# A fused block on one core: TensorE's first phase issued in traced order, with timed tasks between wide projection steps

## The chip, the core and the metric

The kernel runs on one core of a Trainium2 chip, in fp32. The metric is the device time of one execution in microseconds, lower is better. The kernel before takes 3127.56 us (median of 3 runs, 3127.19 to 3137.98).

## What is computed

One decoder block on x (2048 tokens by 1024 channels). The input is RMS-normed and modulated, then multiplied by one large input matrix. Its output feeds a convolution branch and a recurrent branch (RWKV-7), which are projected, gated, merged, projected once more and added to the residual.

```python
h = _rmsnorm(x, norm_g) * (1.0 + scale) + shift
p = h @ w_in                      # 1024 -> 73 tiles of 128 columns
c_val, c_gate, c_og, ts, r_og, g_conv, g_rwkv = split(p)
# convolution branch: causal depthwise width 31, channel LayerNorm, swish
u = layernorm(conv31(c_val * sigmoid(c_gate)) + b)
y_conv = (silu(u) * silu(c_og)) @ w_conv_out
# recurrent branch, 16 heads of 64; token shift, then per token
state = state * w_t - (state @ kk_t) b_t + v_t k_t ;  o_t = state @ r_t
y_rwkv = ((groupnorm(o) + bonus) * silu(r_og)) @ w_rwkv_out
m = sigmoid(g_conv) * y_conv + sigmoid(g_rwkv) * y_rwkv
x = x + gate * (m @ w_out);  return _rmsnorm(x, final_g)
```

## The kernel before

**Tiling.** Tokens go in four blocks of 512 (`TB`). A tile of the input projection is 128 output channels by 512 tokens, eight k-steps of 128 input channels. Every fp32 operand is split into a high and a low half; a k-step (`mm3k`, L188) multiplies high by high, high by low and low by high, and `msplit` cuts the 512 columns in two, so it issues six matmuls of 256 columns. Weight tiles come through six buffers (`load_w`, L165): in block 0 the raw tile is loaded and split by ACT (L178) and GpSimd or DVE (L180), and both halves go back to DRAM; later blocks load the halves (L171, L172). All loads are issued by SP, in order.

**First phase.** For each block there are four groups of four heads. A group has two *pairs* (`pair`, L446): decay products (L455 to L461), cumulative decays (L466), three projections K, R, V with token shift (`shifted`, L413), key norms (L493), the 64x64 decay-and-key products (L523, masked by DVE at L526 and scaled at L532), transposes (L539, L555) and a head sum (`headsum`, L272). Then the *group* (L560) inverts 32x32 triangles: DMAs take the diagonal pieces out (L581, L586), GpSimd solves them (L595, L597), DMAs bring them back (L601, L608), DVE transposes them (L624), and TensorE fills in the off-diagonal quarters (L636, L640). Then comes the *recurrence*, eight chunks of 64 tokens: TensorE L690, DVE L692, TensorE L697, DVE L710, TensorE L714, DVE L717, which writes the state that the next chunk's L690 reads. A group norm (L734 to L743) and transposes (L748) close the group. Around it lie the convolutions (`conv`, L768: two projections and 31 DVE taps, L783), the gates (`gates`, L787: four kinds of one projection each), and `xnorm` (L323), which norms and transposes the next block's input. In the last block, work of the second phase for block 0 takes the place of `xnorm` (`z_first`, `lnorm_first`).

**Second phase.** Per block: output projections of both branches (`rproj`, `cproj`, with 512 columns per matmul, `MS2`), LayerNorm (`lnorm`), the last projection (L1071 to L1073) and the final norm. Block 0's `rproj` and `cproj` run while the last recurrence ends.

**Order.** The code traces a group's pair steps in the order `ORD`, with gates and convolutions before or behind them (`FIRST`, `NEXT`, and `LP` for the last block, which keeps part of the gates for after the last group). The order in which each engine's queue is filled comes from a planner, which runs the traced program in a time model. `high_priority(HP)` lets an instruction pass others in it; `issue_after` pins a few matmuls behind one another. Queues run in the planned order.

Of the kernel before, what the change touches and what calls it, by code (L numbers as in the profile page):

```python
# [18 lines left out]
P = 128  # L19
# [12 lines left out]
KRB, TKB, ASB = 4, 3, 4  # L32
HP = 3000
WDVE, WSH = 6, 0
# [5 lines left out]
VVT, SHT, RKT, RHT, YT = "r", "sh", "k", "sh", "y"  # L40
ORD = (0, 0, 1, 0, 1, 1)
# [3 lines left out]
MS, MS2 = 2, 1  # L45
WB = 6
KEPT = ("in",)
def lplan(t):
    n = {"c": 0, "g": 0}
    r = []  # L50
    for part in t.split():
        l = []
        for w in part:
            if w != "-":
                l.append(("1234" if w == "g" else w, n[w]))
                n[w] += 1
        r.append(l)
    return r


G4 = "1234"
FIRST = (("1", 0), ("2", 0), ("3", 0), ("4", 0), ("c", 0), ("c", 1), (G4, 1))
NEXT = (("c", 0), ("1342", 0), ("c", 1), ("1342", 1))
FILL0 = (0, 1, 0, 0, 0, 0)
LP = "cgcg cgcg cc ccgg gg"
# [17 lines left out]
def hybrid_block(ctx: ExitStack, tc: tile.TileContext, x, vecs, convk, w2a2, final_g, ada, w_in, w_co, w_ro, w_o, crow, out,  # L83
# [55 lines left out]
    msplit = [MS]  # L139

# [24 lines left out]
    def load_w(name, n, hl=None):  # L165
# [10 lines left out]
        wcount[0] -= 1  # L176
        with tc.high_priority(HP):
            nc.scalar.copy(hi, st)  # L178
            lo_eng = nc.vector if wcount[0] >= 0 or (wcount[0] < -1000 and wcount[0] % 4 < W2) else nc.gpsimd
            lo_eng.tensor_tensor(out=lo, in0=st, in1=hi.bitcast(F32), op=ALU.subtract)  # L180
# [17 lines left out]
    def mm3(ps, w, a):  # L198
        for k in range(KT):
            mm3k(ps, w, a, k)  # L200

# [32 lines left out]


# [36 lines left out]
    def headsum(ps, full, hi):  # L272
        lo = e1.tile([P, TB], F32R, name="s_lo", tag="s_lo")
        nc.gpsimd.tensor_tensor(out=lo, in0=full, in1=hi.bitcast(F32), op=ALU.subtract)
        nc.tensor.matmul(ps, bones, hi, start=True, stop=False)
        nc.tensor.matmul(ps, bones, lo, start=False, stop=True)
# [46 lines left out]
    def xnorm(b, tts=range(NTT)):  # L323
        for tt in tts:
# [12 lines left out]
            for kh in range(2):  # L337
                nc.vector.tensor_scalar(out=xh[kh], in0=xh[kh], scalar1=rs, scalar2=None, op0=ALU.mult)
                pt = pl.tile([P, 4, P], F32, name="late", tag="late")
# [73 lines left out]
    def shifted(h, ti, dst):  # L413
        mi = ti - T_R
        ps = front.pop(ti, None)
        if ps is None:
            w = load_w("in", ti)
            ps = pm.tile([P, TB], F32, name="ps_main", tag="main")
            mm3(ps, w, h)
# [7 lines left out]
        nc.vector.tensor_copy(carry[:, mi:mi + 1], ps[:, TB - 1:TB])  # L427
# [18 lines left out]
    def pair(b, q_, pr, h, lora, uv, Asb, rn, res):  # L446
# [4 lines left out]
        for i in range(2):  # L451
            sl = slice(64 * i, 64 * i + 64)
            nc.gpsimd.tensor_tensor(out=wlo[sl, i, :], in0=wf[sl, i, :], in1=wl[sl, i, :].bitcast(F32), op=ALU.subtract)
        pw = pa.tile([P, TB], F32, name="aux", tag="aux")
# [20 lines left out]
        yield  # L475
# [3 lines left out]
        k = e1.tile([P, TB], F32, name="k", tag="k")  # L479
        shifted(h, T_K + pr, k)  # L480
# [3 lines left out]
        E24 = E2.rearrange("p (c e t) -> p c e t", e=2, t=CH)  # L484
        for e in range(2):
            nc.vector.scalar_tensor_tensor(out=KR[:, :, CH * (1 + e):CH * (2 + e)], in0=k4[:, :, e, :],
                                           scalar=vc("rwkv_k_k", pr), in1=E1x[:, :, e, :], op0=ALU.mult, op1=ALU.mult)
        sq = e1.tile([P, TB], F32, name="sq", tag="sq")
        nc.scalar.activation(sq, k, AF.Square, scale=vc("rwkv_k_k", pr))

# [17 lines left out]
        r = e1.tile([P, TB], F32, name="r", tag="r")  # L508
        shifted(h, T_R + pr, r)
# [4 lines left out]
        yield  # L514

        for c4 in range(NCH // 4):
            pA = [pa.tile([P, 2, 256], F32, name="aux", tag="aux") for _ in range(2)]
# [7 lines left out]
            for hh in range(2):  # L525
                nc.vector.tensor_tensor(  # L526
                    out=Asb[:, hh, c4 * 4:c4 * 4 + 4, :].rearrange("p (a e) n -> p a (e n)", e=2),
                    in0=pA[hh], in1=flat(maskA).unsqueeze(1).broadcast_to([P, 2, 256]), op=ALU.mult)
        for e in range(2):
# [3 lines left out]
                [64, 2, NCH // 2, CH]), op=ALU.mult)  # L533

        vv = e1.tile([P, TB], F32, name="vv", tag=VVT)
        shifted(h, T_V + pr, vv)
# [5 lines left out]
        pb = pa.tile([P, TB], F32, name="aux", tag="aux")  # L542
        rh = e1.tile([P, TB], F32R, name="rh", tag=RHT)
        nc.scalar.copy(rh, rk)
        headsum(pb, rk, rh)
        nc.scalar.copy(rk, pb)  # L546
# [3 lines left out]
        tk = l3.tile([P, NCH, P], F32, name="tk", tag="tk", bufs=TKB)  # L550
        for c4 in range(NCH // 4):
            pt = pa.tile([P, 4, P], F32, name="aux", tag="aux")
            for c in range(4):
                cc, e = (c4 * 4 + c) // 2, c % 2
                nc.tensor.transpose(pt[:, c, :], BK[:, cc, e * 128:e * 128 + 128], ident)  # L555
            nc.scalar.copy(tk[:, c4 * 4:c4 * 4 + 4, :], pt)
        res.update(KR=KR, tk=tk, pe=pe)
        yield

    def group(b, g, h, lora, fill):  # L560
        uv = l3.tile([P, NCH, 2, P], F32, name="uv", tag="uv", bufs=2)
        for e in range(2):
            nc.gpsimd.memset(uv[prow(e), e::2], 0.0)
        As = [l3.tile([P, 2, NCH, P], F32, name="As", tag="As", bufs=ASB) for _ in range(2)]
        R = [{}, {}]
        rn = lt.tile([P, 2, NCH // 2, 2], F32, name="rn", tag="rn")
        pairs = [pair(b, q, 2 * g + q, h, lora, uv, As[q], rn, R[q]) for q in range(2)]
        for i, q in enumerate(ORD):
            next(pairs[q])
            fill(i)  # L570


# [45 lines left out]

        pq = [p_.tile([P, 2, 2, NCH // 2, 32], F32, name=n_, tag=n_) for p_, n_ in ((pl, "late"), (pa, "aux"))]
        for e in (1, 0):  # L620
            lo_, hi_ = quarters(e)
            for q in range(2):
                for hh in range(2):
                    nc.vector.transpose(T11[lo_, q, hh], As[q][lo_, hh, e::2, lo_])  # L624
        def turns(mul):

            mm = []
            for n, (q, hh, c) in enumerate(every[::-1]):
                for e in range(2):
                    with tc.issue_after(mm[-1].ins) if mm else nullcontext():  # L630
                        mm_ = mul(e, q, hh, c, dict(start=(n == 0), stop=(n == 15), skip_group_check=True))
                    mm = mm if n else mm + [mm_]

        def lower(e, q, hh, c, kw):
            lo_, hi_ = quarters(e)
            return nc.tensor.matmul(pq[e][hi_, q, hh, c, :], As[q][lo_, hh, 2 * c + e, hi_], T11[lo_, q, hh, c, :], **kw)  # L636

        def upper(e, q, hh, c, kw):
            lo_, hi_ = quarters(e)
            return nc.tensor.matmul(pq[e][lo_, q, hh, c, :], Qs[hi_, q, hh, c, :], As[q][hi_, hh, 2 * c + e, hi_], **kw)  # L640

        turns(lower)
        for e in (1, 0):
            lo_, hi_ = quarters(e)
            nc.vector.tensor_copy(Qs[hi_], pq[e][hi_])

        turns(upper)
        for e in range(2):
            lo_, hi_ = quarters(e)
            for q in range(2):  # L650
                nc.vector.tensor_copy(As[q][lo_, :, e::2, hi_], pq[e][lo_, q])

# [3 lines left out]

# [24 lines left out]
        xcopy(0)  # L681
        for c in range(NCH):
# [4 lines left out]
            for q in range(2):  # L687
                nc.scalar.mul(Se[:, q, :], Sg[:, q, :], R[q]["pe"][:, c:c + 1])  # L688
            for q in range(2):
                nc.tensor.matmul(b_[:, q, :], R[q]["KR"][:, cc, es], Sg[:, q, :], start=(q == 0), stop=False,  # L690
                                 skip_group_check=True)
            nc.vector.tensor_tensor(out=Xz[pr_, e], in0=b_[pr_, 0:2], in1=Xz[pr_, e], op=ALU.add)  # L692


            for n, (q, hh, hs) in enumerate(every):
                with tc.issue_after(mm.ins) if n else nullcontext():
                    mm_ = nc.tensor.matmul(b_[pr_, q, hs], As[q][:, hh, c, kcol(e)], Xz[:, e, q, hs],  # L697
                                           start=(n == 0), stop=(n == 3), skip_group_check=True)
                mm = mm if n else mm_
                if c + 1 < NCH:  # L700
                    with tc.issue_after(mm.ins):
                        xval(c + 1, n)
            if c:
                with tc.issue_after(mm.ins):
                    olast(c - 1)
            if c + 1 < NCH:
                xcopy(c + 1)
            if c:
                ocopy(c - 1)
            nc.vector.tensor_tensor(out=uv[pr_, c].rearrange("p q (h n) -> p q h n", n=64),  # L710
                                    in0=b_[pr_, 0:2].rearrange("p q (h n) -> p q h n", n=64),
                                    in1=rn[pr_, :, cc, :].unsqueeze(3).broadcast_to([64, 2, 2, 64]), op=ALU.mult)
# [3 lines left out]
            for q, hh, hs in every:  # L716
# [434 lines left out]
```

## Time and profile before

| what | value |
|---|---|
| median of the runs | 3127.56 us |
| profiled execution: span, first to last instruction | 3118.7 us |
| profiled execution: its own total time | not listed apart; the runs' median is 8.9 us above the span |
| mean granted TensorE clock | 0.959 |
| busy shares | TensorE 93%, its weight loads 87%, DVE 69%, GpSimd 38%, ACT 32% |
| first phase, by the last input projection | to 2496 us |
| DMA | 667.81 MB, mean 214 GB/s |

The profile shows one execution. A row of the windows gives a stretch (from:to, in us), its length, each engine's busy time with its number of instructions, the granted clock (1.00 is full), the DMA engines' busy share and GB/s. A row of the groups gives line, engine, operation, output and inputs, shapes and count, then busy us, mean ns of one, and the idle time before them with what ended it. A row of the timeline starts with start and duration in us. A row of the waits names who waited for whom: us in total, times, longest. Overlapping matmuls make a busy TensorE look fuller than its rate is.

### The profile page before, as it was taken

The page shows a single profiled execution, that of the slowest core. Times are in us where ns is not written, and L with a number is a line of the kernel's source. Part 1 is how long each engine was busy: PE and PEld are TensorE (multiplying, and loading weights), DVE is VectorE, ACT ScalarE, POOL GpSimd, SP SyncE. Part 2 cuts the span into 40 slices and gives each one's busy share as a digit, 9 for nine tenths or more (in the row PEclk, how much of TensorE's full clock was granted, in tenths as well). Part 3 has the DMA queues.
Part 4 walks back from the last instruction along what each step waited for, and adds up shares of the span by engine and source line. Part 5 has one row for each costly group of instructions (what it writes and reads, how often), then busy time and mean ns, then how long its engine had stood idle before and what let it go on. Part 6 is the DMA issues. An engine that isn't in the chain of part 4 may idle for free.

```text
span 3118.7 us, 65148 instructions
## 1 busy us (share of the span) xinstructions
PE 2902.9 (93%) x25648; PEld 2724.8 (87%) x25648; DVE 2152.8 (69%) x4282; ACT 998.4 (32%) x1932; POOL 1170.4 (38%) x1739
## 2 busy tenths in 40 slices
PE   6789898999999989999999999999979998699998
PEld 6689898899999989899999899999979977578888
DVE  6678775686867767767677677768698446777433
ACT  4324333333333233323332424232333123343211
POOL 3265554343343425232424334416346015634000
PEclk9899999899999989999999999999989999899999
DMA  7666757474756566547565767647437668767664
GB/s 299 215 234 218 262 198 265 153 255 143 237 169 218 167 225 213 190 149 230 154 231 183 243 197 248 221 146 232 151 121 248 220 228 301 275 246 265 213 223 176
DMA packets 354852, 667.81 MB, mean 214 GB/s; under 512 B 134705, under 2 KB 153457, under 8 KB 354545
## 3 DMA queue, kind: packets, MB, share of 16 engines
q1 hardware_dynamic: 354544, 663.64, 63.3%
q8 instruction: 202, 3.31, 0.4%
q14 instruction: 106, 0.86, 0.1%
HBM read 483.07 MB, written 179.31 MB: 212 GB/s over the span
## 4 chain that ended last, share of the span: by engine, by line
PE 52%; DVE 15%; DMA 15%; POOL 8%; issue 4%; SPq 3%; ACT 3%; POOLq 0%; DVEq 0%; ACTq 0%
PE ps_main L195 37%; DMA w_st<-w_in_t 3%; PE aux L523 3%; POOL TT L597 3%; POOL itmp L595 3%; DVE acc L783 2%; DVE M L466 2%; SPq L608 2%; DMA La<-dA 1%; PE xo L697 1%; DMA dT<-TT 1%; PE pout L1072 1%; PE pout L1073 1%; PE xo L714 1%; PE pout L1071 1%
## 5 line engine op out<-in xcount | busy, mean ns | idle before, releaser
L195 PE MATMUL ps_main<-h_hi,w_hi 128*128 128x256 f32 x4608 | 961.0, 287 | 31.6 <-ACT w_hi L178 20.9
L195 PE MATMUL ps_main<-h_hi,w_lo 128*128 128x256 f32 x4608 | 964.0, 287 | 12.8 <-POOL w_lo L180 8.4
L195 PE MATMUL ps_main<-h_lo,w_hi 128*128 128x256 f32 x4608 | 965.0, 287 | 0.0
L195 PEld LDWEIGHTS ps_main<-h_hi,w_hi 128*128 128x128 f32 x4608 | 724.3, 192 | 42.3 <-ACT w_hi L178 22.2
L195 PEld LDWEIGHTS ps_main<-h_hi,w_lo 128*128 128x128 f32 x4608 | 724.3, 191 | 25.1 <-POOL w_lo L180 10.7
L195 PEld LDWEIGHTS ps_main<-h_lo,w_hi 128*128 128x128 f32 x4608 | 725.1, 192 | 8.2 <-issue 0.5
L783 DVE SCALAR_TENSOR_TENSOR acc<-u,ck,acc 128x512 f32<-128x512 f32 x928 | 698.1, 752 | 21.8
L595 POOL TENSOR_TENSOR itmp<-La,TT 128x126 f32<-128x126 f32 (+22 forms) x496 | 179.3, 361 | 162.7 <-DMA La<-dA 126.4
L717 DVE SCALAR_TENSOR_TENSOR S<-xo,pe,Se 64x64 f32<-64x64 f32 x512 | 144.5, 282 | 99.6 <-PE xo L714 90.4
L178 ACT CAST w_hi<-w_st 128x1024 fp32r<-128x1024 f32 x103 | 108.0, 1049 | 323.7 <-DMA w_st<-w_in_t 167.0
L597 POOL TENSOR_TENSOR TT<-TT,itmp 128x126 f32<-128x126 f32 (+22 forms) x496 | 188.8, 381 | 37.3
L180 POOL TENSOR_TENSOR w_lo<-w_st,w_hi 128x1024 fp32r<-128x1024 f32 x47 | 113.0, 2404 | 113.6 <-ACT w_hi L178 100.5
L547 POOL TENSOR_TENSOR vv<-rk,vv 128x512 f32<-128x512 f32 x32 | 42.1, 1316 | 295.4 <-ACT rk L546 295.4
L688 ACT ACTIVATE Se<-S,pe 128x128 f32<-128x128 f32 x256 | 88.9, 394 | 187.6 <-DVE S L717 187.3
L668 ACT COPY Xz<-xo 64x256 f32<-64x256 f32 x128 | 46.8, 365 | 263.2 <-PE xo L673 229.5
L523 PE MATMUL aux<-KR,BK 64*128 64x128 f32 x1024 | 126.1, 308 | 4.4 <-DVE As L526 3.5
L180 DVE TENSOR_TENSOR w_lo<-w_st,w_hi 128x1024 fp32r<-128x1024 f32 x56 | 75.3, 1344 | 75.8 <-ACT w_hi L178 35.7
L710 DVE TENSOR_TENSOR uv<-xo,rn 64x256 f32<-64x256 f32 x128 | 53.8, 420 | 100.5 <-PE xo L697 90.3
L523 PEld LDWEIGHTS aux<-KR,BK 64*128 64x128 f32 x1024 | 102.5, 203 | 20.2 <-DVE As L526 3.6
L526 DVE TENSOR_TENSOR As<-aux,maskA 128x512 f32<-128x512 f32 x128 | 84.1, 687 | 42.4 <-PE aux L523 41.7
L690 PE MATMUL xo<-S,KR 128*128 128x128 f32 x512 | 101.0, 291 | 5.6 <-DVE S L717 3.8
L692 DVE TENSOR_TENSOR Xz<-xo,Xz 64x256 f32<-64x256 f32 x128 | 53.7, 420 | 75.3 <-PE xo L690 70.4
(296 smaller groups left out, 5562.9 us busy)
## 6 DMA issues: line engine op xcount, KB each, us to landing
w_hi<-kh_in SPq DMA_DIRECT2D x219, 512.0 KB, 3.8
w_lo<-kl_in SPq DMA_DIRECT2D x219, 512.0 KB, 5.1
w_st<-w_in_t SPq DMA_DIRECT2D x73, 512.0 KB, 4.8
kh_in<-w_hi SPq DMA_DIRECT2D x71, 512.0 KB, 3.1
kl_in<-w_lo SPq DMA_DIRECT2D x71, 512.0 KB, 4.7
w_hi<-kh_ro SPq DMA_DIRECT2D x32, 512.0 KB, 3.8
w_lo<-kl_ro SPq DMA_DIRECT2D x32, 512.0 KB, 5.1
w_st<-w_co_t SPq DMA_DIRECT2D x32, 512.0 KB, 3.8
```

The source lines that it names most:

```text
L178: nc.scalar.copy(hi, st)
L180: lo_eng.tensor_tensor(out=lo, in0=st, in1=hi.bitcast(F32), op=ALU.subtract)
L195: nc.tensor.matmul(ps[:, qs], ww[:, k, :], aa[k][:, qs], start=(k == 0 and t == 0 and q == 0), stop=(k == KT - 1 and t == 2 and q == ms - ...
L466: nc.vector.tensor_tensor_scan(out=M[:, cs], data0=one, data1=M[:, cs], initial=0.0, op0=ALU.add, op1=ALU.add)
L523: nc.tensor.matmul(pA[hh][:, c // 2, es], BK[hs, cc, es], KR[hs, cc, es], start=(c == 0), stop=(c == 3), skip_group_check=True)
L526: nc.vector.tensor_tensor(out=Asb[:, hh, c4 * 4:c4 * 4 + 4, :].rearrange("p (a e) n -> p a (e n)", e=2), in0=pA[hh], in1=flat(maskA).unsqu ...
L595: nc.gpsimd.tensor_tensor(out=tmp[:, :ni, :nt], in0=La[:, j:j + 1, j + 1:].broadcast_to([P, ni, nt]), in1=TT[:, :ni, j:j + 1].broadcast_to ...
L597: nc.gpsimd.tensor_tensor(out=TT[:, :ni, j + 1:], in0=TT[:, :ni, j + 1:], in1=tmp[:, :ni, :nt], op=ALU.add)
L688: nc.scalar.mul(Se[:, q, :], Sg[:, q, :], R[q]["pe"][:, c:c + 1])
L690: nc.tensor.matmul(b_[:, q, :], R[q]["KR"][:, cc, es], Sg[:, q, :], start=(q == 0), stop=False, skip_group_check=True)
L717: nc.vector.scalar_tensor_tensor(out=Sg[hs, q, hs], in0=b_[hs, 2 + q, hs], scalar=R[q]["pe"][hs, c:c + 1], in1=Se[hs, q, hs], op0=ALU.mult ...
L783: nc.vector.scalar_tensor_tensor(out=acc if i + 1 < HALO else yj, in0=u[:, i:i + TB], scalar=ck[:, j, i:i + 1], in1=acc, op0=ALU.mult, op1 ...
```

## The change

In the first phase and until block 0 of the second is projected, TensorE's queue now has the order in which the program is traced (`manual_schedule`); the other queues are still planned. The trace is made by a small clock: every k-step of a projection advances it by 0.684 us (`US_K`) and then calls every task that is due. Pairs, groups, `xnorm` and the conv taps are such tasks: a `yield a, b` says that the matmuls just traced take `a` us and that the task goes on no sooner than `b` us later; a `yield` of a condition waits for it; `free` holds tasks back while a group's solve products use two PSUM banks. `drain` lets the clock jump when something must be finished first.

A `slot` (one group) traces the input norm, K, R and V of both pairs, and the fixed list `FILL` of convolutions and gates; the previous groups' recurrence goes on among them. In blocks 1 to 3 a convolution comes ahead of the first pair. The last recurrence goes on during block 0's `rproj` and `cproj`. Projections use 512 columns per matmul in the first phase too (`MS = 1`). The low weight halves go to DVE while a group's solve is traced, else to GpSimd (before: the first six after a group). Recurrence operations on DVE and ACT get the high priority. There is a fourth `tk` buffer, `vv` has a tile of its own, and the head sum's low half is made earlier. `LP`, `FIRST`, `NEXT`, `ORD` and most `issue_after` are gone.

```diff
-KRB, TKB, ASB = 4, 3, 4
+KRB, TKB, ASB = 4, 4, 4
-WDVE, WSH = 6, 0
-VVT, SHT, RKT, RHT, YT = "r", "sh", "k", "sh", "y"
-ORD = (0, 0, 1, 0, 1, 1)
+VVT, SHT, RKT, RHT, YT = "vv", "sh", "k", "sh", "y"
-MS, MS2 = 2, 1
+MS = 1
-FIRST = (("1", 0), ("2", 0), ("3", 0), ("4", 0), ("c", 0), ("c", 1), (G4, 1))
-NEXT = (("c", 0), ("1342", 0), ("c", 1), ("1342", 1))
-LP = "cgcg cgcg cc ccgg gg"
+FILL = ("c", "1", "3", "4", "2", "c", "1", "3", "4", "2")
+US_MM, US_K = 0.228, 0.684
...
-            lo_eng = nc.vector if wcount[0] >= 0 or (wcount[0] < -1000 and wcount[0] % 4 < W2) else nc.gpsimd
+            lo_eng = nc.vector if lo_dve[0] or (name != "in" and wcount[0] % 4 < W2) else nc.gpsimd
...
     def mm3(ps, w, a):
         for k in range(KT):
             mm3k(ps, w, a, k)
+            tick(US_K)
...
+        def step(self):
+            try:
+                r = next(self.gen)
...
+            if callable(r):
+                self.cond = r
+            else:
+                self.cond = None
+                now[0] += r[0]
+                self.at = now[0] + r[1]
...
+    def tick(us):
+        now[0] += us
+        poll()
+
+    def drain(*ts):
+        poll()
+        while not all(t.done for t in ts):
+            at = [t.at for t in tasks if t.at > now[0] and (t.cond is None or t.cond())]
+            now[0] = min(at)
+            poll()
...
+            yield 0.0, 18.0
+                yield 0.6, 3.5
...
+        yield 0.0, G.wait
+        yield 0.0, 3.0
+        yield 0.0, 4.5
+            yield 1.2, 2.6
...
+        lo_dve[0] = True
+        yield 0.0, 35.0
+        lo_dve[0] = False
+        yield 0.0, 25.0
+        yield lambda: G.pairs == 2 and (before is None or before.done)
+        with tc.issue_after(lastv[0].ins):
+        yield 0.0, 4.5
...
+            yield 0.6, 2.0
+            yield 1.1, 2.0
+            yield 0.6, 2.8
...
+        yield 0.5, 18.0
...
+            if i % 2:
+                yield 0.0, 2.0
...
+    def proj(h, ti, name, box):
+        ps = product(h, ti)
+        drain(*pairs_[-2:-1])
+        dst = e1.tile([P, TB], F32, name=name, tag=name)
+        shifted(ps, ti, dst)
+        box[name[0]] = dst
+        poll()
+
+    def slot(b, g, h, lora, first):
+        drain(*side, *groups_[-2:-1])
+        G = opened(b, g, h, lora)
+        if first:
+            G.wait = 8.0
...
+        if b + 1 < NB:
+            side[:] = [Task(xnorm(b + 1, XN[g]))]
+        else:
+            z_first(ZN[g])
+            side[:] = [Task(once(lambda: lnorm_first(g)))] if g < 3 else []
+        groups_.append(Task(group(G, groups_[-1] if groups_ else None)))
...
+        if first and b:
+            fill(1)
+        for q in range(2):
+            box = {}
+            pr = 2 * g + q
+            pairs_.append(Task(pair_after(G, q, box, pairs_[-1] if pairs_ else None)))
+            poll()
+            proj(h, T_K + pr, "k", box)
+            proj(h, T_R + pr, "r", box)
+            proj(h, T_V + pr, "vv", box)
+            fill(2)
+        fill(len(todo))
...
+    with tc.manual_schedule(engines={mybir.EngineType.PE}):
+        for b in range(NB):
+            if b:
+                drain(*side)
+                h = hprep(b)
+            lora = lora_split(h)
+            for g in groups:
+                slot(b, g, h, lora, g == 0)
...
+        drain(*pairs_, *convs)
...
+        rproj(0, lsplit(z_dram), mr)
+        cproj(0, lsplit(u_dram), None)
+        drain(*groups_)
```

More of the change, by code (lines that the diff above doesn't have):

```diff
@@ L338, in xnorm @@
                 nc.vector.tensor_scalar(out=xh[kh], in0=xh[kh], scalar1=rs, scalar2=None, op0=ALU.mult)
+            yield 0.0, 18.0
+            for kh in range(2):
+                yield free
                 pt = pl.tile([P, 4, P], F32, name="late", tag="late")
@@ L411, in hprep0, with product, shifted @@
         return h
-    def shifted(h, ti, dst):
+    def product(h, ti):
+        return front.pop(ti) if ti in front else project(h, ("in", ti))
+    def shifted(ps, ti, dst):
         mi = ti - T_R
[L415 to L419, printed above, removed]
         t1 = e2.tile([P, TB], F32, name="t1", tag="t2", bufs=T2B)
@@ L444, in hybrid_block, with free, pair @@
     kcol, rcol = prow, vrow
-    def pair(b, q_, pr, h, lora, uv, Asb, rn, res):
+    locked = [False]
+    def free():
+        return not locked[0]
+    class Group:
+        pass
+    def pair(G, q_, box):
+        b, pr, lora, uv, Asb, rn = G.b, 2 * G.g + q_, G.lora, G.uv, G.As[q_], G.rn
         wf = e1.tile([P, 2, P], F32, name="wf", tag="wf")
@@ L541, in pair, with opened, group @@
             nc.scalar.copy(uv[vrow(e), e::2, q_, :], pv[vrow(e)])
[L542 to L546, printed above, removed]
         nc.gpsimd.tensor_tensor(out=vv, in0=rk, in1=vv, op=ALU.mult)
         nc.sync.dma_start(bv_dram[b][pr], vv)
[L550 to L561, printed above, removed]
-        for e in range(2):
[L563 to L570, printed above, removed]
+        G.R[q_].update(KR=KR, tk=tk, pe=pe)
+        G.pairs += 1
+        yield 0.5, 0.0
+    def opened(b, g, h, lora):
+        G = Group()
+        G.b, G.g, G.h, G.lora, G.tri, G.pairs, G.wait = b, g, h, lora, 0, 0, 0.0
+        G.uv = l3.tile([P, NCH, 2, P], F32, name="uv", tag="uv", bufs=2)
+        for e in range(2):
+            nc.gpsimd.memset(G.uv[prow(e), e::2], 0.0)
+        G.As = [l3.tile([P, 2, NCH, P], F32, name="As", tag="As", bufs=ASB) for _ in range(2)]
+        G.R = [{}, {}]
+        G.rn = lt.tile([P, 2, NCH // 2, 2], F32, name="rn", tag="rn")
+        return G
+    lastv = [None]
+    def group(G, before):
+        g, b, As, uv, rn, R = G.g, G.b, G.As, G.uv, G.rn, G.R
+        yield lambda: G.tri == 2
         dA = dp.tile([2, 2, NCH // 2, 2, 2, 32, 32], F32, name="dA", tag="dA", bufs=2)
@@ L654, in group @@
+        yield 0.9, 2.5
+        turns(upper)
+        with tc.high_priority(HP):
+            for e in range(2):
+                lo_, hi_ = quarters(e)
+                for q in range(2):
+                    nc.vector.tensor_copy(As[q][lo_, :, e::2, hi_], pq[e][lo_, q])
+        locked[0] = False
+        yield 0.9, 3.0
         O = uv[:, 0::2]
@@ L695, in group @@
+            yield 0.6, 2.0
             for n, (q, hh, hs) in enumerate(every):
[L696 to L699, printed above, removed]
+                nc.tensor.matmul(b_[pr_, q, hs], As[q][:, hh, c, kcol(e)], Xz[:, e, q, hs],
+                                 start=(n == 0), stop=(n == 3), skip_group_check=True)
@@ L923, in hybrid_block @@
-    early.close()
-    if not phase2:
-        late.close()
-        return
-    ob = ctx.enter_context(tc.tile_pool(name="ob", bufs=2, side="right", reuse_waits="tile"))
-    f2 = ctx.enter_context(tc.tile_pool(name="f2", bufs=2, side="right", reuse_waits="tile"))
-    oa = ctx.enter_context(tc.tile_pool(name="oa", bufs=1, side="right", reuse_waits="tile"))
-    def split(hi, lo, src, eng):
-        nc.scalar.copy(hi, src)
-        eng.tensor_tensor(out=lo, in0=src, in1=hi.bitcast(F32), op=ALU.subtract)
@@ L988, in hybrid_block, with once @@
-    mr = mnew()
-    rproj(0, lsplit(z_dram), mr)
-    cproj(0, lsplit(u_dram), None)
-    mhi, mlo = okt(0)
-    for n in range(KT):
-        split(mhi[n], mlo[n], mr[n], nc.vector)
+    def once(f):
+        yield free
+        f()
+    pairs_, groups_, side = [], [], []
+    def proj(h, ti, name, box):
[5 more added lines that the diff above has]
+        poll()
@@ new lines, in slot, with fill @@
+    def slot(b, g, h, lora, first):
[3 more added lines that the diff above has]
+            G.wait = 8.0
+        if b in (1, 2):
+            for _ in range(2):
+                n_ = later.pop(0)
+                for half in range(2):
+                    presplit(*n_, half)
+        if b + 1 < NB:
[4 more added lines that the diff above has]
+        groups_.append(Task(group(G, groups_[-1] if groups_ else None)))
+        cj, gj = [2 * g, 2 * g + 1], {w: [2 * g, 2 * g + 1] for w in "1234"}
+        todo = list(FILL)
+        def fill(n):
+            for _ in range(n):
+                w = todo.pop(0)
+                if w == "c":
+                    conv(b, h, cj.pop(0))
+                else:
+                    gates(b, h, gj[w].pop(0), w)
+        if first and b:
+            fill(1)
+        for q in range(2):
+            box = {}
[7 more added lines that the diff above has]
+        fill(len(todo))
```

323 lines of the change are left out of this document (171 added, 152 removed).

## The prediction, made before the result was known

> **What bounds the kernel now.** I began with the page, for engine shares and slices, then cut the span into stages, then looked inside a good and a bad stretch.
>
> ```profile
> span 3118.7 us, 65148 instructions
> PE 2902.9 (93%) x25648; PEld 2724.8 (87%) x25648; DVE 2152.8 (69%) x4282; ACT 998.4 (32%) x1932; POOL 1170.4 (38%) x1739
> PE   6789898999999989999999999999979998699998
> PEclk9899999899999989999999999999989999899999
> PE 52%; DVE 15%; DMA 15%; POOL 8%; issue 4%; SPq 3%; ACT 3%; POOLq 0%; DVEq 0%; ACTq 0%
> ```
>
> TensorE is the bound: 93% busy and half of the chain that ended last. But the page does not say at what rate it works when busy. The windows by stage do: after the times comes the busy time of each engine with its number of instructions, and then the granted clock. The stages are the start, up to the first recurrence of block 1, then of block 2, of block 3, the rest of the first phase, the change of phase, the second phase.
>
> ```profile
> 0.00:100.00 100.00, 69.29 (x464) 64.46 (x464) 70.20 (x168) 47.55 (x85) 36.68 (x41) 0.93 0.74 275
> 100.00:850.00 750.00, 691.80 (x6564) 660.68 (x6564) 550.18 (x1056) 264.79 (x472) 331.46 (x489) 0.94 0.65 219
> 850.00:1459.00 609.00, 576.92 (x5566) 552.72 (x5564) 431.88 (x877) 186.73 (x386) 220.11 (x394) 0.96 0.60 194
> 1459.00:2036.00 577.00, 563.04 (x5518) 539.15 (x5519) 415.37 (x857) 180.80 (x370) 223.50 (x393) 0.98 0.64 211
> 2036.00:2480.00 444.00, 421.77 (x4146) 403.26 (x4145) 326.12 (x651) 135.61 (x261) 188.48 (x307) 0.96 0.57 187
> 2480.00:2720.00 240.00, 199.46 (x1202) 170.20 (x1202) 143.65 (x247) 71.89 (x143) 101.09 (x68) 0.91 0.75 264
> ```
>
> From 100 to 2480 us TensorE issues 6564+5566+5518+4146 = 21,794 matmuls in 2380 us, or 9.16 per us. It is idle 2380-2253.5 = 126.5 us of that. Smaller windows show what it can do, and what happens where it can't:
>
> ```profile
> 600.00:1000.00 400.00, 387.54 (x3863) 374.58 (x3862) 303.26 (x602) 131.64 (x258) 157.26 (x279) 0.99 0.63 206
> 2000.00:2200.00 200.00, 197.53 (x2032) 190.97 (x2032) 151.75 (x310) 59.37 (x114) 82.70 (x131) 1.00 0.60 198
> 900.00:1000.00 100.00, 99.17 (x995) 96.56 (x995) 75.72 (x141) 25.84 (x53) 38.60 (x83) 1.00 0.67 216
> 1140.00:1150.00 10.00, 7.59 (x64) 7.11 (x62) 2.79 (x14) 4.08 (x10) 0.00 (x0) 1.00 0.68 235
> 1150.00:1160.00 10.00, 6.38 (x132) 4.75 (x132) 5.83 (x12) 4.25 (x9) 4.27 (x5) 0.53 0.61 196
> 1160.00:1170.00 10.00, 5.31 (x42) 4.40 (x44) 8.67 (x14) 3.32 (x6) 8.17 (x10) 0.50 0.34 108
> ```
>
> Good stretches run 9.66 (600 to 1000), 9.95 (900 to 1000) and 10.16 per us (2000 to 2200) at a clock of 0.99 to 1.00. Between 1140 and 1170 us the projections have run out: TensorE goes through transposes, the 32x32 solve, decay products and the next recurrence, each waiting for ACT or DVE, and is half idle; the clock falls to 0.5. Such holes lie once per block. They, and not the mass of matmuls, are what order can recover.
>
> By the Trainium skill ("TensorE: Matmul & The Clock Gate", Part 1) an idle window of about 3.4 us halves the clock until a busy window has passed. The 0.53 and 0.50 above agree.
>
> **The change, part by part.** First, the columns. A projection's k-step now issues three matmuls of 512 columns instead of six of 256. Both widths stand in the trace, the wide one in the second phase:
>
> ```profile
> 2420.09 0.40 PE L195 MATMUL ps_main<-h_lo,w_hi 128*128 128x256 f32 x2
> ...
> 2423.86 0.40 PE L195 MATMUL ps_main<-h_hi,w_lo 128*128 128x256 f32 x2
> 2911.69 0.39 PE L195 MATMUL ps_main<-u_hi,w_hi 128*128 128x512 f32 x1
> ...
> 2915.32 0.39 PE L195 MATMUL ps_main<-u_lo,w_hi 128*128 128x512 f32 x1
> 2562.54 0.40 PE L195 MATMUL ps_main<-o_lo,w_hi 128*128 128x512 f32 x1
> ...
> 2567.68 0.40 PE L195 MATMUL ps_main<-o_hi,w_lo 128*128 128x512 f32 x1
> L195 PE MATMUL ps_main<-h_hi,w_lo 128*128 128x256 f32 x4608 | 964.0, 287 | 12.8 <-POOL w_lo L180 8.4
> ```
>
> A pair of halves takes (2423.86-2420.09)/16 = 0.2356 us. One wide matmul takes 3.63/16 = 0.2269 us on u_hi, 5.14/22 = 0.2336 us on o_hi. There are 3 x 4608 narrow ones, so 6912 pairs: the gain is between 14 us (o_hi's rate) and 60 us (u_hi's). I see no reason why h should follow the one or the other and take the middle, 37 us, all of it on the path.
>
> The Trainium skill gives a fixed 2.5 ns per warm matmul ("TensorE: Matmul & The Clock Gate", section "Wait — 56ns, not 53.3ns?"). By that estimate the columns would bring 6912 x 2.5 ns = 17 us and the sum would be 20 us smaller; the rows stand against it, at the nearer end.
>
> Second, the order. Until now a planner ordered TensorE's queue; now it issues as traced, and the trace weaves recurrence, pair preparation, norm transposes and solve in between k-steps as tasks. A group's recurrence lies behind the next slot's 18 projections, block 1 to 3 open with a convolution that covers the lora step, and each conv lets other DVE work in after two taps. So the holes get projections. If all 21,794 matmuls went at 9.66 per us, they would take 2256 us, 124 less than now; at 9.95, 2190 us, 190 less; at 10.16, 2145 us, 235 less. I take the middle of the first two, 157 us: these rates are held for 100 to 400 us now, and a fixed order cannot do better everywhere. The start (0 to 100 us) keeps its code and its time.
>
> What of the other engines is on that path? A wait in the traced order stops everything behind it on TensorE, the projections too. A recurrence step hands over three times (L690 to L692, L697 to L710, L714 to L717); the trace leaves 2.0, 2.0 and 2.8 us before the consumer is issued.
>
> ```profile
> L783 DVE SCALAR_TENSOR_TENSOR acc<-u,ck,acc 128x512 f32<-128x512 f32 x928 | 698.1, 752 | 21.8
> L717 DVE SCALAR_TENSOR_TENSOR S<-xo,pe,Se 64x64 f32<-64x64 f32 x512 | 144.5, 282 | 99.6 <-PE xo L714 90.4
> L692 DVE TENSOR_TENSOR Xz<-xo,Xz 64x256 f32<-64x256 f32 x128 | 53.7, 420 | 75.3 <-PE xo L690 70.4
> DVE uv L710 <- PE xo L697: 90.3, 55, 4.7
> DVE S L717 <- PE xo L714: 90.4, 50, 3.7
> DVE Xz L692 <- PE xo L690: 70.4, 37, 5.8
> ```
>
> One tap in front costs 0.752 us and the operation itself 0.420: 1.17 us, inside 2.0. Four state updates take 4 x 0.282 = 1.13, with a tap 1.88, inside 2.8. So with at most one tap ahead, a handover costs TensorE nothing.
>
> The solve goes by way of DMA and GpSimd. The trace allows 35+25 us for it:
>
> ```profile
> 895.60 1.40 DVE L532 TENSOR_TENSOR As<-As,rn 64x512 f32<-64x512 f32 x2
> ...
> 950.56 0.61 DVE L624 STREAM_TRANSPOSE T<-As 32x128 f32<-32x128 f32 x2
> SPq L171 <- PE ps_main L195: 693.4, 178, 9.3
> ```
>
> From L532's end to the last L624 it takes 54 us here, so 60 covers it, narrowly. Its DMAs are issued by SP, behind weight loads that wait for a buffer up to 9.3 us; one such wait too many would show on TensorE. I count nothing for it; 9 us in each of 16 groups would be 144 us and bring the forecast to the second rival.
>
> The rest I cost at nothing: low halves of weights stay about as they were divided between DVE and GpSimd; a fourth tk buffer and vv's own tile free waits; the early split for the head sum is the same work, beside projections.
>
> Third, the end of the phase. The last block no longer holds gates back for the last recurrence.
>
> ```profile
> 2462.96 0.61 PE L690 MATMUL xo<-S,KR 128*128 128x128 f32 x4
> 2495.59 0.40 PE L195 MATMUL ps_main<-h_hi,w_lo 128*128 128x256 f32 x2
> 2599.55 0.77 ACT L750 ACTIVATE oc<-late,hgb,hgg 128x512 f32<-128x512 f32 x1
> 2702.24 0.80 PE L195 MATMUL ps_main<-m_hi,w_hi 128*128 128x512 f32 x1 [23.48 <-DVE mr L984]
> ```
>
> Now the last recurrence starts 33 us before the last input projection and its output is normed 104.7 us after it; the next block's output projection follows 102 us later, partly cold (0.91 in the stage's row). In the new order about ten projections (56 us) follow the decay products' start, the solve takes 60 us from some 9 us later, and the recurrence about 110 us (eight steps of 9.8 us, which is 2.3 us of own matmuls and the three delays rounded up to k-steps of 0.684 us, plus solve products and norm). It ends near 120 us after the last input projection: about 15 us later, 0 to 40. The 16 projections of block 0's second phase (90 us) hide most of the rest.
>
> Sum: 37 + 157 - 15 = 179 us saved. The profiled execution spans 3118.7 us; the runs' median, 3127.56, is 8.9 us more, launch and end around it, which don't change. 3127.6 - 179 = 2949.
>
> **Rivals.** *More of both (13%).* Order holds 10.16 per us throughout, and h runs at u_hi's rate: 235 + 60 - 0 = 295 us, 2833. For it: two blocks already have such stretches. Against: block 0 also has weights to split, at a DMA share of 0.65 in its row.
>
> *Columns only (14%).* The holes move instead of closing, because the pair preparation stays DVE-bound (the 1160 row: DVE 8.67 of 10). Gain 14 to 60, less 0 to 40 for the end: about 3105, between 3068 and 3127 and a little over.
>
> *TensorE waits in order (13%, slower).* The place is the recurrence's handovers, 3 x 8 x 16 = 384. In only 37+55+50 = 142 did DVE stand waiting for the result; in 242 it was still at other work. DVE is busy 76% of the good stretches and more if the phase shrinks: 1723 us of work (the four rows) in 2190 is 79%. If three taps stood ahead (2.26 + 0.42 = 2.68), each wait would exceed the 2.05 us of three k-steps by 0.63 us: 384 x 0.63 = 242 us, and the balance is 63 us slower, 3190. It decides from 179/384 = 0.47 us per handover. Against it: recurrence operations carry a high priority and the taps come in twos. By the Trainium skill's clock rule named above, stalls over 3.4 us would cost more still; none of these waits is that long.
>
> **How the numbers follow.** Forecast 60%; its own range is 2878 (190 + 60, nothing lost at the end) to 3030 (124 + 14 - 40). The 8-in-10 range, 2825 to 3115, takes in the better case and most of columns-only and leaves out the slower one. A measurement tells 0.5% (16 us) from nothing: faster holds the forecast, the better case and 9 of the 14 points of columns-only, 82%; no change 5%; slower 13%.
>
> **What would show it.** Right: ps_main rows of 128x512 x2304 per term, spaced 0.227 to 0.234; PEclk of 9 without a dip once per block; a block of the first phase in about 545 us (137 per group) instead of the 609 and 577 of the rows above; TensorE idle between 100 us and the phase's end under 60 us. Wrong: waits of L697, L714 or L690 for DVE, or of L636 for the solve, adding up to over 100 us, with PEclk dips spread over all slots; or the first output projection of the second phase over 240 us after the last input projection.

## The result, and the profile after

The changed kernel takes 3077.24 us (median of 4 runs, 3070.85 to 3086.55) beside 3127.38 us: ratio 0.983, 95% interval 0.981 to 0.985, or 50 us less. The direction of the prediction held, and the time lies in its wide range, 2825 to 3115 us; the size, 179 us, and the forecast's own range, 2878 to 3030, did not come. Its page begins so:

```profile
span 3074.4 us, 50973 instructions
PE 2806.0 (91%) x18640; PEld 2292.0 (75%) x18640; DVE 2092.9 (68%) x4279; ACT 1003.0 (33%) x1932; POOL 1183.6 (38%) x1742
PE   6879898986999999789999998999999999799998
PEclk9989999998999999899999999999999999899999
L180 PE MATMUL ps_main<-h_hi,w_hi 128*128 128x512 f32 x2304 | 966.3, 419 | 27.1 <-ACT w_hi L163 14.5
```

The columns are there (x2304 per term), and TensorE issues 7008 fewer matmuls. The share of its busy time fell from 93 to 91%: what is gone was partly busy time, and idle time grew. The waits of TensorE, longest first in total, say where:

```profile
PE late L371 <- DVE xt L365: 49.4, 2, 27.7
PE xo L766 <- DVE Xz L762: 23.0, 22, 3.0
PE ps_main L180 <- DVE mr L1100: 18.5, 2, 15.9
PE late L819 <- POOL uv L812: 18.3, 3, 10.9
```

The last column is the longest wait of the line. L371, the norm's transposes, has only two, but of 27.7 and 21.7 us. The windows from 100 us to the last input projection give the sum, first before, then after:

```profile
100.00:2496.00 2396.00, 2269.53 (x21939) 2171.49 (x21940) 1727.79 (x3453) 771.13 (x1496) 963.55 (x1582) 0.96 0.62 205
100.00:2436.60 2336.60, 2154.09 (x14840) 1734.57 (x14838) 1649.56 (x3403) 771.70 (x1487) 967.54 (x1586) 0.97 0.64 208
```

TensorE idles 182.5 us there instead of 126.5. The stage is 59.4 us shorter; from the last input projection to the end it is 15.1 us longer (622.8 us before, 637.9 after). 59.4 - 15.1 = 44.3, the difference of the two spans.

One of the two long waits, in the timeline of TensorE, DVE and SP:

```profile
687.76 0.60 PE L782 MATMUL xo<-uv,tk 128*128 128x128 f32 x4
...
693.91 0.42 SPq L139 DMA_DIRECT2D w_st<-w_o_t  x1
694.42 0.41 SPq L142 DMA_DIRECT2D w_gr<-grow_d  x1
...
700.70 0.42 SPq L357 DMA_DIRECT2D xt<-x_in  x1
...
706.54 0.16 DVE L361 TENSOR_TENSOR ss<-ss 128x1 f32<-128x1 f32 x1 [4.60 <-ACT xsq L358]
706.62 0.75 DVE L866 SCALAR_TENSOR_TENSOR acc<-u,ck,acc 128x512 f32<-128x512 f32 x1
707.27 0.15 DVE L362 TENSOR_SCALAR ss<-ss 128x1 f32<-128x1 f32 x1
...
715.44 0.88 DVE L365 TENSOR_SCALAR xt<-xt,ss 128x512 f32<-128x512 f32 x2
716.07 1.09 PE L371 MATMUL late<-ident,xt 128*128 128x128 f32 x4 [27.70 <-DVE xt L365]
717.38 0.63 PE L180 MATMUL ps_main<-h_lo,w_hi 128*128 128x512 f32 x1
717.81 0.63 PE L180 MATMUL ps_main<-h_hi,w_lo 128*128 128x512 f32 x1
```

In blocks 1 and 2 a slot traces `presplit` (four half tiles of weights to be loaded, split and stored for later, L139 to L148) ahead of the input norm. The norm's loads (L357) stand behind it on SP and in the shared `hx` buffers, and go out at 700.70. But its transposes have their place in TensorE's queue, 18 us after the norm began by the trace's clock, and every projection behind them waits. Afterwards matmuls start 0.43 us apart instead of 0.23, at half clock. DVE adds to the wait: from 706.54 to 715.44 the norm's small operations alternate with eleven conv taps of 0.76 us, some 8 of the 27.7 us. The other norms of block 1 have their loads out 20 to 110 us ahead of their transposes (for instance at 754 us for 864), and none makes TensorE wait like this.

### The profile page after: what moved, and what is told of

The parts are those of the page before. It is cut to its first block, busy times and chain, and to the rows that moved or that the text cites. A ratio compares the mean times of both kernels' runs of the same rounds, so it can differ in the third digit from the quotient of the medians.

```text
span 3074.4 us, 50973 instructions
## 1 busy us (share of the span) xinstructions
PE 2806.0 (91%) x18640; PEld 2292.0 (75%) x18640; DVE 2092.9 (68%) x4279; ACT 1003.0 (33%) x1932; POOL 1183.6 (38%) x1742
## 4 chain that ended last, share of the span: by engine, by line
PE 40%; DVE 15%; DMA 8%; POOL 6%; issue 4%; SPq 2%; ACT 1%; POOLq 0%; DVEq 0%; ACTq 0%
PE ps_main L180 27%; DVE acc L866 5%; PE pout L1187 2%; PE pout L1186 2%; PE pout L1188 2%; DMA w_st<-w_ro_t 1%; POOL TT L655 1%; POOL itmp L653 1%; PE aux L569 1%; DMA w_gr<-grow_d 1%; PE xo L766 1%; SPq L666 1%; PE xo L740 1%; DVE S L786 1%; PE xo L782 1%
## 5 line engine op out<-in xcount | busy, mean ns | idle before, releaser
L180 PE MATMUL ps_main<-h_hi,w_hi 128*128 128x512 f32 x2304 | 966.3, 419 | 27.1 <-ACT w_hi L163 14.5
L180 PE MATMUL ps_main<-h_hi,w_lo 128*128 128x512 f32 x2304 | 918.9, 399 | 12.4 <-DMA w_lo<-kl_in 4.8
L180 PE MATMUL ps_main<-h_lo,w_hi 128*128 128x512 f32 x2304 | 915.6, 397 | 0.2 <-DVE h_lo L385 0.2
L180 PEld LDWEIGHTS ps_main<-h_hi,w_hi 128*128 128x128 f32 x2304 | 442.5, 192 | 121.5 <-ACT w_hi L163 16.4
L180 PEld LDWEIGHTS ps_main<-h_hi,w_lo 128*128 128x128 f32 x2304 | 440.2, 191 | 120.7 <-POOL w_lo L165 7.6
L180 PEld LDWEIGHTS ps_main<-h_lo,w_hi 128*128 128x128 f32 x2304 | 442.7, 192 | 80.1 <-DVE h_lo L385 1.4
L766 PEld LDWEIGHTS xo<-Xz,As 128*64 128x64 f32 x1024 | 69.6, 138 | 70.4 <-DVE Xz L762 38.4
L450 ACT ACTIVATE t<-ps_main,mu 128x512 f32<-128x512 f32 x96 | 65.9, 686 | 136.5 <-PE ps_main L180 133.9
L766 PE MATMUL xo<-Xz,As 128*64 128x64 f32 x1024 | 87.4, 229 | 23.2 <-DVE Xz L762 23.0
L847 POOL COPY u<-tail 128x30 f32<-128x30 f32 x32 | 10.2, 322 | 251.5 <-DVE yj L866 237.7
```

The source lines that it names most:

```text
L180: nc.tensor.matmul(ps[:, qs], ww[:, k, :], aa[k][:, qs], start=(k == 0 and t == 0 and q == 0), stop=(k == KT - 1 and t == 2 and q == ms - ...
L450: nc.scalar.activation(t1, ps, AF.Identity, scale=mu1[:, mi:mi + 1])
```

## The experiments

The first two ask which half of the change works, the next two what the waits cost. **Columns alone**, in the planned order:

```diff
-MS, MS2 = 2, 1
+MS, MS2 = 1, 1
```

> The kernel before with 512 columns per matmul in its first phase, its planned order kept otherwise. Theory (the columns carry the whole gain, the traced order nothing net): h's wide matmuls start 0.2295 us apart in the changed kernel against 0.2356 for a pair of halves, 6912 x 0.0061 = 42 us, so 3085, between 3075 and 3100. Rival (the order carries it, and in a planned order wide matmuls only make short ones wait longer): 3115 to 3135.

It takes 3338 us, 1.065 (1.062 to 1.068): my theory fell, and so did the rival. Wide columns in the planned order cost 205 us (3338.4 beside 3133.6 on the same chip). The windows of the tile ps_main alone, each over one recurrence, count the projection matmuls in it: before and in this kernel (both the last group of block 1), then in the changed kernel (first group of block 2):

```profile
1310.00:1393.00 83.00, 59.36 (x421) 53.34 (x419) 5.88 (x12) 5.21 (x8) 0.96 0.42 132
1427.00:1523.00 96.00, 70.96 (x290) 53.27 (x290) 7.02 (x13) 5.57 (x9) 0.99 0.46 141
1465.00:1543.00 78.00, 55.03 (x205) 38.13 (x204) 4.57 (x9) 5.05 (x8) 0.96 0.59 192
```

Before, 421 halves, or 210 wide ones, lie in a recurrence of 83 us. In the columns-only kernel it is 290 wide ones in 96 us: the planner puts more projections between a recurrence's handovers, so the recurrence is slower and the projections run out earlier. Over all 16 recurrences, each from its first state product (L690, L757) to its last, the mean is 212 wide ones in 84 us before, 289 in 104 us here, and 200 in 78 us in the changed kernel. When projections run out, this happens, here twice at a group's end (windows with all instructions again, of the columns-only kernel):

```profile
1222.00:1269.00 47.00, 20.90 (x218) 15.68 (x217) 20.99 (x51) 18.87 (x40) 18.90 (x20) 0.60 0.47 140
1883.00:1925.00 42.00, 20.25 (x211) 15.49 (x212) 19.75 (x52) 18.24 (x40) 15.18 (x18) 0.55 0.52 166
```

Between 100 us and the last input projection, stretches of over 4 us without a projection matmul add up to 155 us in 11 places before, to 609 us in 35 places here, and to 145 us in 17 places in the changed kernel; TensorE's idle time there is 126.5, 291 and 182.5 us. The changed kernel's own clock charges 0.684 us per k-step and puts 205 in 78 us. Why the planner fills in more is not known; its prices were not looked into.

**Order alone**, the changed kernel with halves in its first phase:

```diff
-MS = 1
+MS = 2
...
+        msplit[0] = 1
         mr = mnew()
```

> The changed kernel with its first phase cut back to two matmuls of 256 columns. Theory (columns carry the gain): 3077 + 42 = 3119, level with before within 0.5%. Rival (order carries it): 3080 to 3095.

3097.8 us, 0.989 (0.986 to 0.992): by the ratio 34 us faster than before. Neither number came: both halves of the change gain, 34 us by order, and 18 more by columns (0.983 against 0.989). To see in what, I took for each matmul the time from its start to the next one's, less the next one's wait, from 100 us to the last input projection (us; from the traces):

```
                        before  order only  after  e10 (halves)  e11 (wide)
projections             1727.6    1707.7   1680.3     1717.4       1683.8
decay products           111.7      70.3     71.6       73.4         71.7
other pair work          117.2     104.3    102.8      103.0        102.8
recurrence               247.0     239.1    240.4      243.0        240.9
solve products            42.9      37.0     36.4       37.1         37.0
norms and the rest        23.1      22.4     22.5       22.6         22.5
idle                     126.5     168.3    182.5      146.5        149.9
length                  2396.0    2349.4   2336.6     2343.2       2308.5
```

The order makes the stage 46.6 us shorter. The work shrinks by 88 us, of which 41 in the decay products; part of the rest is clock (TensorE works about 150 us at half clock before, about 86 with the order). And idle time grows by 42; the norm's two waits alone are 52.8 in this run. Now the **norm ahead of the presplit**, whose halves the edit also spaces 4 us apart:

```diff
-        if b in (1, 2):
-            for _ in range(2):
-                n_ = later.pop(0)
-                for half in range(2):
-                    presplit(*n_, half)
...
-            side[:] = [Task(xnorm(b + 1, XN[g]))]
+            def normed(b=b, g=g, todo_=todo_):
+                yield from xnorm(b + 1, XN[g])
+                for n_, half in todo_:
+                    presplit(*n_, half)
+                    yield 0.0, 4.0
+            side[:] = [Task(normed())]
```

> The changed kernel, with the splitting of later weights (presplit) traced behind the next block's input norm instead of ahead of it. Theory (the order's gain was eaten by two places, 27.7 and 21.7 us long, where TensorE stands in front of the norm's transposes because the norm's loads lie behind eight weight halves on SP and in the shared buffers): those 49 us of waits go, and some of the half clock behind them, 3077 - 50 = 3027, between 3015 and 3045. Rival (DVE sets the pace, and the wait turns up at the next in-order handover): 3065 to 3080, with the 49 us found on other lines.

3048.3 us, 0.973 (0.970 to 0.975), 29 us faster than the change. The line's wait falls as foreseen:

```profile
L371 PE MATMUL late<-ident,xt 128*128 128x128 f32 x96 | 15.0, 280 | 12.2 <-DVE xt L365 10.3 <-DVE As L718 1.9
```

39 of 51 us of it are gone, and the stage is 28 us shorter; the other 11 turned up in the projections (more half clock) and elsewhere. That the presplit ahead of the norm caused most of the two waits is shown; what came back, 29 us, is less than the 50 foreseen.

**Longer delays** at the other waits; beside those shown, 3.0 became 3.7 (key norm), and 4.5 became 5.2 and 5.9 (ahead of the decay and the solve products):

```diff
-            yield 0.6, 2.0
+            yield 0.6, 2.7
-        yield 0.5, 18.0
+        yield 0.5, 24.0
```

> The changed kernel with longer delays where TensorE was seen waiting in order: Xz 2.0 to 2.7 us, group norm 18 to 24, key norm 3.0 to 3.7, ahead of the decay products 4.5 to 5.2, ahead of the solve products 4.5 to 5.9. These places hold 23 + 18 + 10 + 14 + 12 = 77 us of waits. Theory (the delays are a little short): half of it goes, about 3045. Rival (the waits are not short delays but single mishaps of a late buffer or load; a longer recurrence only costs): 3070 to 3085.

3071.4 us, 0.980 (0.977 to 0.983), which overlaps the change's own: the rival's number. TensorE's idle time in the stage did not fall (185.1 us beside 182.5). The waits moved:

```profile
PE late L371 <- DVE xt L365: 53.7, 2, 29.4
PE late L819 <- POOL uv L812: 17.6, 2, 17.4
PE ps_main L180 <- DMA w_lo<-kl_in: 17.6, 6, 5.1
PE xo L782 <- DVE uv L777: 14.7, 11, 6.1
PE xo L766 <- DVE Xz L762: 12.6, 9, 4.0
```

Xz fell from 23.0 to 12.6 us; the next handover, uv, rose from 6.7 to 14.7, and a weight load from 4.8 to 17.6.

Then, why the decay products became cheaper. **Pinned** in the kernel before:

```diff
-                    nc.tensor.matmul(pA[hh][:, c // 2, es], BK[hs, cc, es], KR[hs, cc, es], ...)
+                    with tc.issue_after(dp_.ins) if c or hh else nullcontext():
+                        dp_ = nc.tensor.matmul(pA[hh][:, c // 2, es], BK[hs, cc, es], KR[hs, cc, es], ...)
```

> The kernel before, with the sixteen decay products of a pair's half pinned one behind another in the order in which they are traced (head 0, head 1, head 0, ...). Theory (a part of the order's gain is that products of head 0, on partitions 0 to 63, and of head 1, on 64 to 127, overlap when they stand next to each other, which the planned order broke up: 126 us of busy time on that line before, 79 after): the line falls to about 80 us and the time by 30 to 45 us, to 3090. Rival (the 47 us were waits for what feeds them, and turn up elsewhere): 3120 to 3135.

3100.2 us, 0.991 (0.989 to 0.994): 31 us faster, but not by the mechanism alone, since the line fell only to 113.6 us (projections still stand between the pairs) and the planner's whole order moved with the pins. **Heads apart** in the changed kernel is the clean test:

```diff
-            for c in range(4):
-                for hh in range(2):
+            for hh in range(2):
+                for c in range(4):
```

> The changed kernel, with the decay products traced head 0 first and then head 1, so that neighbours use the same 64 partitions. Theory (overlap of the two heads): 1024 products at about 0.108 us instead of 0.070 on average, 39 us more: 3116, and a busy time of the line near 120 us. Rival (the gain came from fewer interruptions, not from the neighbours): 3077, line near 80 us.

3109.1 us, 0.994 (0.992 to 0.996): 32 us slower than the change, and the theory holds. Timeline rows of sixteen products each, two of the changed kernel, then two with the heads apart, and the line in all:

```profile
1451.87 1.16 PE L569 MATMUL aux<-KR,BK 64*128 64x128 f32 x16
1003.68 1.16 PE L569 MATMUL aux<-KR,BK 64*128 64x128 f32 x16
```

```profile
1012.70 1.71 PE L569 MATMUL aux<-KR,BK 64*128 64x128 f32 x16
1016.99 1.71 PE L569 MATMUL aux<-KR,BK 64*128 64x128 f32 x16
L569 PE MATMUL aux<-KR,BK 64*128 64x128 f32 x1024 | 115.5, 294 | 16.4 <-POOL KR L552 8.1 <-POOL BK L546 7.6 <-DVE As L718 0.6
```

0.55 us per sixteen, 64 times, is 35 us. The line before and after:

```profile
L523 PE MATMUL aux<-KR,BK 64*128 64x128 f32 x1024 | 126.1, 308 | 4.4 <-DVE As L526 3.5 <-ACT ta L463 0.5 <-POOL BK L506 0.4
L569 PE MATMUL aux<-KR,BK 64*128 64x128 f32 x1024 | 79.1, 292 | 16.0 <-POOL KR L552 6.8 <-DVE carry L456 3.7 <-POOL BK L546 3.2
```

By the Trainium skill ("TensorE: Matmul & The Clock Gate", Part 3, on packing small matmuls) matmuls on different rows of the array run at the same time, their starts about 4 ns apart. The traces agree, with a slightly larger step: in the changed kernel a product starts 7 ns after its neighbour on the other 64 rows, and some 105 ns after one on the same. That the planned order had broken up such pairs stands in the traces too: of the products followed directly by another one, 265 of 907 had it start within 20 ns before, 456 of 958 after.

**Half the taps** asks whether DVE's queue sets the pace:

```diff
-        for i in range(HALO):
+        for n, i in enumerate(range(0, HALO, 2)):
```

> e3_norm_ahead with every second conv tap left out (15 instead of 30 per tile, so the convolution is another one): 480 x 0.752 = 361 us less work on DVE. Theory (what is left of TensorE's waits is in-order handovers of many kinds, of which DVE's queue is one part): TensorE's idle time falls by the Xz, uv, S and half of the other DVE waits, 30 to 50 us, so about 3005. Rival (DVE's queue sets the pace of the traced order): 80 us or more, below 2970. Second rival (DVE does not matter): 3040 to 3050.

3027.8 us, 0.968 (0.964 to 0.971): about 20 us below its own base, for 361 us less work on DVE. None of the three numbers came. TensorE's idle time in the stage falls from 145.6 to 137.9, its wait for Xz from 20.8 to 13.0, and that for the norm from 10.3 to 5.3. DVE's queue costs something, but it does not set the pace.

**The end**, with the last pair ahead of the last gates:

```diff
             proj(h, T_V + pr, "vv", box)
-            fill(2)
+            if not (b == NB - 1 and g == 3):
+                fill(2)
```

> e3_norm_ahead, with the last group's second pair traced ahead of that slot's convolutions and gates, so that the last solve and recurrence start some three projections (17 us) earlier. Theory (the end after the last input projection is longer by 15 us because the last recurrence starts later): 10 to 17 us faster than e3_norm_ahead, about 3035. Rival (the end waits for the loads and splits of block 1's second phase): no change, 3048.

3054.0 us, 0.977 (0.974 to 0.979): no gain, the rival's number. The last recurrence's output is out 108.8 us after the last input projection instead of 128.8, but that projection ends 7 us later and the span stays (3051.6 against 3052.4). TensorE's longest wait behind it, for DVE's `mr` (L1107 there, L1108 here), is 13.8 us instead of 16.9. What else the end waits for was not followed.

Last, **the columns' own worth**, without the long waits, the kernel of the norm ahead with halves and with wide columns on one chip:

> e3_norm_ahead with its first phase cut back to two matmuls of 256 columns, beside e11_wide, the same with 512. Theory A (the columns bring what the spacing says, 6912 x 0.0061 = 42 us, and the 18 us between e2_order_only and the changed kernel were lost in the two long stalls): 40 us slower than e11_wide, 3090. Theory B (part of what the projections gain is waited away at the handovers, since recurrence, decay products and norms take as long as before): 15 to 25 us slower, 3065 to 3075.

> The kernel of e3_norm_ahead once more, on the chip of e10_halves, so that the two can be compared to half a per cent: 3048, and the ratio to the kernel before 0.973.

3070.2 us (0.983, 0.980 to 0.985) and 3047.7 us (0.975, 0.973 to 0.977): 22 us apart, theory B's number, but not clearly by its mechanism. The table shows 33.6 us less time in the projections; the stage is 34.7 us shorter, the profiled spans differ by 29.2 and the medians by 22.5. So little of it is waited away in the stage in these two executions; before the norm was moved, 27 us were gained in the projections and 14 given back as idle time. The kernel with halves also says what the order is worth with the norm moved: a ratio of 0.983 to before, or 54 us.

## Why the prediction was wrong, and where it was right

**The order (157 us) was the step that failed.** With halves kept it is worth 46.6 us in the stage and 34 us in the runs' time, and 54 us with the norm moved. I read the good stretches' rate as one that every stretch could have, laid the difference to the four holes, and did not price them. The longest stretches without projections before begin at 536, 1146, 1757 and 2291 us and last 28.9, 28.5, 15.3 and 33.4 us:

```profile
536.00:565.00 29.00, 16.53 (x206) 12.76 (x207) 17.10 (x48) 13.81 (x27) 11.43 (x13) 0.65 0.62 215
1146.00:1175.00 29.00, 16.68 (x205) 13.24 (x204) 19.37 (x35) 12.41 (x26) 14.47 (x16) 0.58 0.44 142
1757.00:1772.50 15.50, 10.04 (x75) 8.26 (x73) 11.60 (x27) 7.31 (x15) 10.07 (x12) 0.75 0.61 192
2291.00:2325.00 34.00, 19.25 (x218) 14.85 (x217) 32.84 (x68) 9.64 (x16) 9.54 (x12) 0.64 0.23 75
```

TensorE idles 45 us in them, and by the trace's clock record it works 50 us at half clock in them and 19 just behind. With matmuls 0.43 instead of 0.23 us apart at half clock, about half that time is lost, so the holes were worth some 80 us by this estimate, not 157. For 157, nearly four fifths of all that the stage loses would have had to go: 126.5 us of idle time and about 75 by half clock.

The four did close. But two of 29 and 22 us at 688 and 1292 took their place, for a reason that stands in the whole diff: `xnorm` was traced ahead of `presplit` and now is behind it, and I had counted what the norm's transposes cost and not what they queue behind, although I named SP's queue for the solve. A third, 15.5 us at 341, has a wait of 10.9 us of the group's last transposes (L819) for GpSimd. Without the norm's two waits idle time is still 146 us, where the good stretches' 3% would have been 70; the largest wait left is 20.8 us for Xz, in 23 pieces. Neither longer delays nor fewer taps took much of the rest, and what would stays open. And a part of the gain, 36 to 41 us in the decay products, had nothing to do with holes; I had not seen it.

**The columns (37 us) were somewhat over-sized.** h runs between the two rates that I had: seven steps of the changed kernel, from 685.92 to 687.53, are 0.230 us each.

```profile
685.92 0.40 PE L180 MATMUL ps_main<-h_lo,w_hi 128*128 128x512 f32 x1
...
687.53 0.39 PE L180 MATMUL ps_main<-h_hi,w_lo 128*128 128x512 f32 x1
```

By this spacing 6912 pairs would gain 39 us; the projections' own time shrank by 27 to 34 us, the runs by 18 to 23. The estimate of 17 us lay inside the 14 to 60 that I took from the rows, so they did not stand against it, as I wrote; the runs' 18 to 23 are near it, but the spacing, 0.0056 us less for each pair, is not. The rival "columns only" has the result in its span, for a wrong reason: alone they cost 205 us. So it is luck that the wide range, made to take in that rival, holds the result. What the prediction missed is that order and columns hang together.

**The end (15 us) was right in size**, 15.1, but partly by luck. The norm of the last recurrence ends 129.0 us after the last input projection, where I said 120, so 24 us later than before and not 15. And I read a wrong row: the projection at 2702.24 us is not the second phase's first of its kind (that is at 2666.0 us before, 2616.8 after), only the first one behind the 23.48 us wait. Nor are the 8.9 us between span and median launch and end, as I had it: the changed kernel's profiled run took 3076.14 us with a span of 3074.4, so the rest is more likely how executions differ. The sum does not change by it.

**In-order waits (the slower rival)** came at 34 us for all three recurrence handovers (23.0 for Xz, 6.7 for uv, 3.9 for S), not 242. A step of the recurrence, put at 9.8 us, takes 10.4 us (median of the traced ones). The traced order did cost in-order waits, but more in two mishaps than in 384 handovers. Of the marks of being right, the spacing of the wide matmuls held; the others show the forecast wrong: idle time 182.5 us, not under 60; blocks of 598, 604 and 580 us, not 545; and the granted clock still dips at the two long waits (tenth and seventeenth slice of PEclk above).

## What to carry to other kernels

When a queue gets a fixed order, look for each moved instruction at everything that must be done before it can start, on every queue and in every shared buffer, and at what was traced ahead of that: two norms whose loads stood behind four weight halves made TensorE wait 49 us in all, 384 tight handovers 34. Do not take the rate of the best stretches for the rate of all; price the holes one by one, by the idle time and the half clock in them. And an edit that gains beside another can lose alone: here the wider matmul cost 205 us in the planned order and saved 18 to 23 in the traced one, for a reason that was not found.

## What the runs showed of the hardware

Products on 64 partitions each overlap when neighbours use different halves: sixteen take 1.16 us in turns and 1.71 us when each half comes by itself, and breaking such pairs up is a cost that no idle time shows, since TensorE looks busy in both. And the width of a matmul matters little by itself: 512 columns take 0.2356 us as two halves and 0.230 as one.
